# Attention scores whose second pass contracts 128 rows instead of 64

## The chip, the cores and the metric

The kernel runs on one core of a Trainium2 chip. The metric is the device time of one execution in microseconds (us). TensorE (PE) multiplies matrices; a matmul is two records, the load of its stationary operand (PEld, LDWEIGHTS) and the streaming of its moving operand (PE, MATMUL). VectorE (DVE), ScalarE (ACT) and GpSimd (POOL) do the rest, SyncE (SP) issues the weight loads.

## The reference, cut to what matters

Two layers of a diffusion backbone over 256 latent and 256 context tokens of width 1024. Each layer is a half-step SwiGLU feed-forward, a mixer, and another half-step feed-forward. The mixer has three branches on one projected input: grouped-query attention (A, 8 query heads of 64, 2 key heads), differential attention (B, 4 heads with two softmax maps each) and a Fourier mix (C). What the change touches is the scores:

```python
s = jnp.einsum('bqhgd,bkhd->bhgqk', q * HEAD_DIM ** -0.5, k)      # A, HEAD_DIM = 64
s = jnp.einsum('bqhmd,bkhmd->bhmqk', q * HEAD_DIM ** -0.5, k)     # B, two maps m
p = jax.nn.softmax(s, axis=-1)
```

Latent queries see 512 keys (context and latent), context queries see the 256 context keys. In the second layer the context has no queries.

## The kernel before

Every product is made of float32r parts: a float32 value is split into a high part (a cast on ACT) and a low part (a subtraction on DVE), and `mm3` (lines 305 to 307) multiplies high by high, high by low and low by high. Weights come through a stream (`WeightStream`, lines 202 and 203) that loads them and splits them ahead of their use.

The mixer's work on TensorE stands in an order written out at build time. `Interleave` keeps a clock of its own: large products (projections of six units, gates, branches) are run in the order of `PACE[l]["order"]`, and between them it puts the stages of small tasks whose operands its clock calls ready. Each stage yields its time on TensorE, its time on VectorE and a delay to the next stage (`sa`, `sb`, `tr`, ... in `PACE`). TensorE takes the result strictly in that order, so a stage that is put too early makes all products behind it wait.

Attention runs in units: two of branch A (4 query heads and 1 key head each) and four of branch B (2 query maps and 2 key maps each). `unit_post` normalises q and k, applies the rotation, and for each of the four token tiles of 128 writes two packs: pq has a query head as 128 columns [high, low] (in B's second map [low, high]), pk has a key head as [high, high] (`dup`), and after these the low part of k, 64 columns for each key head (`low`, line 651). Each pack of 128 columns is transposed on TensorE into a PSUM bank `att` (line 660) and copied by ACT (line 662) into a slot of the unit's stack, so that the 128 rows of a slot hold a head's 64 dimensions twice. The low part is transposed on its own (line 665): in A it has 64 columns and gives 64 rows, in B two heads of 64 columns give the two halves of 128 rows. A copy of its own on ACT (line 666) follows.

`scores` makes the scores of 128 queries and 512 or 256 keys in pairs of matmuls. The first (line 679) contracts 128 rows, [q high; q low] with [k high; k high]; the second (line 680) adds q high times k low and contracts the 64 rows in which q high lies:

```python
nc.tensor.matmul(d, qt, k, start=True, stop=False)                 # line 679
nc.tensor.matmul(d, qt[rows], low[rows], start=False, stop=True)   # line 680
```

Then DVE takes the negated maximum (line 683), ACT the exponential with its sum (line 686), DVE the reciprocal (line 687) and the scaling (line 710 in A; lines 746 to 748 in B). `spread` transposes the result (line 698), ACT and DVE split it into parts (lines 263 and 264), and TensorE multiplies it with v (line 723 in A, `mm3` in B).

Of the kernel before, what the change touches and what calls it, by code (L numbers as in the profile page):

```python
# [32 lines left out]
# z ** -0.5 on [0.9324, 1.0691], where the guess puts z, as a polynomial with the leading coefficient scaled to 1  # L33
# [29 lines left out]
class Slots:  # L63
    """buffers that a task holds over several of its stages"""
# [14 lines left out]
class Stack:  # L79
    """a unit's transposed operands: eight slots of the latent and the context tokens, in one buffer or in two"""  # L80
# [11 lines left out]
    def keys(self, i, half):  # L92
        """all keys that a query of half sees, in pieces"""
        if half == 1:
            return [self.half(i, 1)]
        return [self.half(i, 0), self.half(i, 1)] if self.whole is None else [self.whole[:, i, :]]
# [8 lines left out]
class Interleave:  # L105
    """Puts the stages of small tasks between the products of large ones, in the order in which their operands
    are due: a stage yields its time on TensorE and on VectorE, and the delay to the next; a large one the times
    alone, or the tasks that it needs."""
# [62 lines left out]
class WeightStream:  # L171
    """Weight pieces in the order of their use: loads of whole pieces and splits of their halves into two
    float32r parts run ahead."""
# [32 lines left out]
    def next(self, key):  # L206
        """the two parts of the next half of a piece, to be given back with done()"""
        i = self.used
        assert self.pieces[i // 2][0] == key, (self.pieces[i // 2][0], key)
        self.ahead()  # L210
        assert self.split > i
        self.used += 1
        return self._parts(i)[1:]
# [6 lines left out]
class Net:  # L220
# [37 lines left out]
    def region(self, tag, dt, name):  # L258
        """a shared 16 KB region for a new use"""
        return self.pool.tile([P, 8, 512], dt, name=f"{tag}_{name}", tag=tag)  # L260
# [5 lines left out]
    def urgent(self, on=True):  # L266
        """ahead of what was emitted shortly before"""
        return self.tc.high_priority(offset=URG) if on else nullcontext()

    def rsqrt(self, y, x, sums, n, t):  # L270
        """1 / sqrt(sums / n + EPS): a first guess from the exponent, then a polynomial in x * guess ** 2"""
        v = self.nc.vector
        v.tensor_scalar(x, sums, RSQRT_SCALE / n, RSQRT_SCALE * EPS, op0=ALU.mult, op1=ALU.add)
        v.tensor_scalar(y.bitcast(I32), x.bitcast(I32), -0.5, RSQRT_MAGIC, op0=ALU.mult, op1=ALU.add)
        v.tensor_tensor(t, y, y, op=ALU.mult)
        v.tensor_tensor(x, t, x, op=ALU.mult)
        v.scalar_tensor_tensor(t, x, RSQRT_POLY[3], x, op0=ALU.add, op1=ALU.mult)
        for c in RSQRT_POLY[2:0:-1]:
            v.scalar_tensor_tensor(t, t, c, x, op0=ALU.add, op1=ALU.mult)
        v.scalar_tensor_tensor(y, t, RSQRT_POLY[0], y, op0=ALU.add, op1=ALU.mult)  # L280

    def col_rsqrt(self, sq, n, dg):
        """sq [P, 256]: rsqrt(column sum / n + EPS) on all partitions, in PSUM"""
        self.col_scale(sq, n, dg)
        return self.spread_cols(dg)
# [24 lines left out]
    def cond_region(self, name, after=None):  # L310
        """silu of both conditioning vectors on all partitions, and room for the rows of w_ada"""
        nc = self.nc
        t = self.region("ya", F32, name)
        self.sil = t[:, 0:4, :].rearrange("p (c a) b -> p c (a b)", c=2)
        self.adaraw = [t[:, 4 + 2 * i:6 + 2 * i, :].rearrange("p a b -> p (a b)") for i in range(2)]
        self.bg_base = 0
        if after is not None:
            nc.gpsimd.tensor_copy(self.sil[:, 0, 0:1], after)
        nc.gpsimd.dma_start(self.sil, self.io["cc"])
        for c in range(2):  # L320
            s, u = self.sil[:, c, :], self.adaraw[c]
            nc.scalar.activation(u, s, AF.Tanh, scale=0.5)
            nc.vector.scalar_tensor_tensor(s, u, 1.0, s, op0=ALU.add, op1=ALU.mult)
# [6 lines left out]
    def bg_plan(self, n):  # L330
        """n rows of w_ada spread evenly over the coming feed-forward"""
        self.bg_n, self.bg_done, self.bg_time = n, 0, 0
        self.bg_total = 512 * (2 * NF + 2 * (KT - 3) + KT)
# [74 lines left out]
    def update(self, m, half, ps, g):  # L408
        """h += gate * ps"""
        c = _half(half)  # L410
        self.nc.vector.scalar_tensor_tensor(self.h[:, m, c], ps[:, c], g[:, m, half:half + 1], self.h[:, m, c],  # L411
                                            op0=ALU.mult, op1=ALU.add)
        self.fin(m, half)
# [140 lines left out]
    def unit_proj(self, l, u, kv_only, run, first, needs, post):  # L554
        """q, k and v of one unit for all token tiles; kv_only: no q for the context"""
# [25 lines left out]
    def unit_post(self, u, ps, c0s):  # L581
# [9 lines left out]
        # values  # L591
        for half in range(2):
            vs = self.raw[half][:, :, nh * HD:384]
            if is_a:
                vd = st.half(6, half).rearrange("p (t x d) -> p t x d", t=2, x=2)
                vd = [vd[:, :, i, :] for i in range(2)]
            else:
                vd = [st.half(5 + i, half).rearrange("p (t c) -> p t c", t=2) for i in range(2)]
            self.split(vd[0], vd[1], vs)
        # queries and keys  # L600
# [13 lines left out]
        kd, kl = (4, 5) if is_a else (2, 4)  # L614
        cost, lat = 7.0, self.pace["post"]
        for half in range(2):
# [16 lines left out]
            # transposed stacks: q [hi; lo], k [hi; hi], lo of k  # L633
            for tt in range(2):
# [14 lines left out]
                low = pk[:, nk * P:nk * P + nk * HD]  # L649
                nc.scalar.copy(dup, ks.unsqueeze(2).to_broadcast([P, nk, 2, HD]))  # L650
                nc.vector.tensor_tensor(low.rearrange("p (a d) -> p a d", d=HD), ks, _r(dup[:, :, 0, :]), op=ALU.subtract)
                cols += [(kd + i, pk[:, i * P:i * P + P]) for i in range(nk)]
                yield 0.0, cost, lat
                cost, lat = 0.5, self.pace["tt"]
                pe = (len(cols) + 1) * 0.08
# [7 lines left out]
                b = self.att.next()  # L663
                m = nk * HD
                nc.tensor.matmul(b[:m, 0:P], low, self.identr, start=True, stop=True)
                nc.scalar.copy(st.tok(kl, half, tt)[:m], b[:m, 0:P])
# [3 lines left out]
    def scores(self, half, st, q, kd, kl, rows, e, qts):  # L670
        """exp(S - max) [P q, keys] of query tiles qts, and 1 / sum; q, kd, kl: slots of st"""
# [3 lines left out]
        for x, i in enumerate(qts):  # L675
            qt, o = st.tok(q, half, i), x * n
            for k, low in zip(st.keys(kd, half), st.keys(kl, half)):
                d = ps[:, o:o + k.shape[-1]]
                nc.tensor.matmul(d, qt, k, start=True, stop=False)  # L679
                nc.tensor.matmul(d, qt[rows], low[rows], start=False, stop=True)  # L680
                o += k.shape[-1]
# [8 lines left out]
    def spread(self, half, es, pt):  # L690
        """transposes es, two [P q, keys], into pt"""
# [9 lines left out]
    def att_a(self, j, half, pr, e):  # L701
        nc = self.nc
        st = self.stack(j)
        rows = slice(0, HD)
# [3 lines left out]
        for x, qts in enumerate(((0,), (1,)) if half == 0 else ((0, 1),)):  # L708
            for p, rc in self.scores(half, st, 2 * pr + e, 4, 5, rows, slots[x], qts):
                nc.vector.tensor_scalar(p, p, rc, None, op0=ALU.mult)  # L710
                es.append(p)
# [14 lines left out]
        # the sum of the rows by the two parts of v  # L726
# [9 lines left out]
    def att_b(self, b, half):  # L736
# [5 lines left out]
        for qts in ((0,), (1,)) if half == 0 else ((0, 1),):  # L742
            slots = yield from self.ep.get(2)
            s = [self.scores(half, st, m, 2 + m, 4, slice(m * HD, m * HD + HD), slots[m], qts) for m in range(2)]
# [15 lines left out]
        for k in range(nk):  # L760
            kc = slice((k % 2) * 256, (k % 2) * 256 + 256)
            v = [st.tok(5 + x, half + k // 2, k % 2) for x in range(2)]
# [23 lines left out]
    def split_tables(self):  # L786
        """position tables in pt (hi 0,1, lo 2,3), channel tables in pt 4 (hi | lo)"""
# [6 lines left out]
    def uc_proj(self, l, halves, hn1):  # L794
        """u of branch C, token-major: hi in u1 0..3, lo in u1 4..7"""
# [24 lines left out]
    def fourier(self, g, half, s):  # L820
        """the sums over positions for the cosines and sines of frequencies 0..128 alone: tokens are ordered so that
        those of 255..128 mirror them"""
# [35 lines left out]
    def branch(self, l, i, y, mp, N, first, last, needs):  # L858
        """adds gate * (y @ w_branch) of two feature tiles to the merged sum"""
# [32 lines left out]
    def gates(self, l, mp, N):  # L892
        """the tanh of two feature tiles of branch B's gates, kept beside the merged sum"""
# [39 lines left out]
    def mixer_steps(self, l):  # L933
        """the large steps in order, with the weight pieces that each takes"""
# [95 lines left out]
    def start(self):  # L1030
        """loads; shift and scale of the first norm as (silu(c) @ w_ada) on the tensor engine"""
# [106 lines left out]
def _order():  # L1138
    """tokens 0..127, then 255..128"""
# [83 lines left out]
```

## Time and profile before

| what | value |
|---|---|
| median of 3 runs | 2172.9 us |
| lowest, highest | 2165.63, 2173.29 us |
| span of the profiled execution | 2166.2 us |
| PE, PEld busy in the span | 2135.8 us, 1819.9 us |
| DVE, ACT, POOL busy | 1486.5, 919.3, 113.8 us |
| matmuls | 11706 |

The profiled execution has no time of its own printed beside its span; the span is 6.7 us (0.3%) under the median of the runs and 0.6 us over the lowest. A line number such as L680 is the line of the kernel above. The start of a matmul is a record, its end is modelled, so two neighbouring matmuls overlap in the records, and the time from one start to the next is what a matmul takes of the engine.

### The profile page before, as it was taken

What the parts mean: (1) busy time and instruction counts of PE and PEld (TensorE: products, weight loads), DVE (VectorE), ACT (ScalarE), POOL (GpSimd) and SP (SyncE); (2) the same over time, 40 slices, a digit from 0 to 9 for tenths busy, and PEclk for the clock granted to TensorE, in tenths of its full rate; (3) what the DMA queues carried; (4) which work ended last, traced back from release to release, by engine and by line L of the source; (5) the groups of instructions that cost most, each with busy time, mean ns of one, the idle gap of its engine ahead of it and who ended that gap; (6) DMA issues with size and microseconds to landing.
All of it is one profiled execution on the core that took longest, in us unless ns stands there. A gap on an engine that the chain in (4) does not pass through costs nothing.

```text
span 2166.2 us, 31632 instructions
## 1 busy us (share of the span) xinstructions
PE 2135.8 (99%) x11706; PEld 1819.9 (84%) x11706; DVE 1486.5 (69%) x3102; ACT 919.3 (42%) x1920; POOL 113.8 (5%) x235
## 2 busy tenths in 40 slices
PE   8999999999999999999999999999999999999999
PEld 3888888898888878888888898888888889988999
DVE  5878777667777774676666568765556687877664
ACT  4323333356654543332333333233324576655553
POOL 2000001100000010000000000000010000000000
PEclk9999999999999999999999999999999899999999
DMA  7545555321112243244544425555553223444655
GB/s 290 190 154 193 172 166 174 94 90 61 59 61 67 81 146 101 68 166 136 165 139 144 145 73 201 175 175 174 167 161 119 83 86 98 134 166 157 186 184 146
DMA packets 84779, 300.49 MB, mean 139 GB/s; under 512 B 9872, under 2 KB 11024, under 8 KB 83088
## 3 DMA queue, kind: packets, MB, share of 16 engines
q1 hardware_dynamic: 62640, 219.29, 31.1%
q0 software_dynamic: 21984, 79.18, 11.7%
q8 instruction: 92, 1.51, 0.3%
q14 instruction: 63, 0.52, 0.1%
HBM read 293.19 MB, written 5.24 MB: 138 GB/s over the span
## 4 chain that ended last, share of the span: by engine, by line
PE 96%; DVE 2%; ACT 1%; DMA 1%; issue 0%; SPq 0%; ACTq 0%; DVEq 0%
PE mm L305 29%; PE mm L306 29%; PE mm L307 28%; PE att L680 2%; PE att L679 2%; PE mm L1056 1%; PE att L698 1%; PE att L660 1%; PE att L723 1%; DVE wlo L203 1%; PE att L299 1%; PE att L307 1%; PE att L305 0%; PE att L306 0%; PE att L291 0%; DMA wraw<-in_wout 0%
## 5 line engine op out<-in xcount | busy, mean ns | idle before, releaser
L202 ACT CAST whi<-wraw 128x512 fp32r<-128x512 f32 (+1 forms) x832 | 497.0, 600 | 919.9 <-PE mm L306 829.2
L203 DVE TENSOR_TENSOR wlo<-wraw,whi 128x512 fp32r<-128x512 f32 (+1 forms) x832 | 548.8, 664 | 360.7 <-ACT whi L202 356.5
L305 PE MATMUL mm<-hn,whi 128*128 128x512 f32 (+1 forms) x1888 | 666.0, 355 | 2.0 <-ACT hn L385 2.0
L306 PE MATMUL mm<-hn,whi 128*128 128x512 f32 (+1 forms) x1888 | 666.5, 354 | 0.0
L307 PE MATMUL mm<-hn,wlo 128*128 128x512 f32 (+1 forms) x1888 | 661.0, 351 | 0.0
L305 PEld LDWEIGHTS mm<-hn,whi 128*128 128x128 f32 x1888 | 355.9, 189 | 59.9 <-ACT hn L385 2.9
L307 PEld LDWEIGHTS mm<-hn,wlo 128*128 128x128 f32 x1888 | 356.7, 189 | 52.0
L306 PEld LDWEIGHTS mm<-hn,whi 128*128 128x128 f32 x1888 | 356.4, 189 | 49.9 <-DVE hn L386 0.2
L305 PE MATMUL mm<-whi,hn 128*128 128x384 f32 (+3 forms) x432 | 147.9, 342 | 0.7 <-DVE mg_m L884 0.6
L307 PE MATMUL mm<-whi,hn 128*128 128x384 f32 (+3 forms) x432 | 143.1, 331 | 0.3 <-DVE hn L386 0.3
L306 PE MATMUL mm<-wlo,hn 128*128 128x384 f32 (+3 forms) x432 | 143.0, 331 | 0.0
L352 DVE CUSTOM_DVE_ANT_0 gt<-ya_c,small 128x1024 bf16<-128x1024 f32 x113 | 142.9, 1280 | 0.0
L352 DVE CUSTOM_DVE_ANT_0 e<-ya_c,small 128x1024 bf16<-128x1024 f32 x111 | 140.5, 1280 | 0.8 <-DMA ya_c<-in_wada 0.8
L348 POOL DMA_DIRECT2D ya_c<-in_wada x128 | 67.8, 529 | 926.7 <-DVE ada L352 905.5
L305 PE MATMUL mm<-u_f,whi 128*128 128x256 f32 (+1 forms) x304 | 101.7, 335 | 0.0
L306 PE MATMUL mm<-u_f,whi 128*128 128x256 f32 (+1 forms) x304 | 101.6, 334 | 0.0
L307 PE MATMUL mm<-u_f,wlo 128*128 128x256 f32 (+1 forms) x304 | 100.7, 331 | 0.0
L411 DVE SCALAR_TENSOR_TENSOR h_h<-mm,gcol,h_h 128x256 f32<-128x256 f32 x104 | 49.9, 482 | 60.6 <-PE mm L307 59.9
L305 PEld LDWEIGHTS mm<-whi,hn 128*128 128x128 f32 x432 | 81.6, 189 | 6.9 <-issue 2.7
L307 PEld LDWEIGHTS mm<-whi,hn 128*128 128x128 f32 x432 | 81.5, 189 | 3.0 <-DVE hn L386 0.8
L306 PEld LDWEIGHTS mm<-wlo,hn 128*128 128x128 f32 x432 | 81.7, 189 | 2.2
L683 DVE TENSOR_REDUCE sm<-att 128x1 f32<-128x512 f32 (+1 forms) x80 | 54.5, 686 | 25.6 <-PE att L680 25.1
(261 smaller groups left out, 3248.3 us busy)
## 6 DMA issues: line engine op xcount, KB each, us to landing
wraw<-in_wi SPq DMA_DIRECT2D x176, 512.0 KB, 3.7
ya_c<-in_wada POOLq DMA_DIRECT2D x128, 512.0 KB, 3.9
wraw<-in_wo SPq DMA_DIRECT2D x64, 512.0 KB, 3.7
wraw<-in_gate SPq DMA_DIRECT2D x48, 512.0 KB, 3.5
wraw<-in_win SPq DMA_DIRECT2D x48, 384.0 KB, 3.1
wraw<-in_wo SPq DMA_DIRECT2D x32, 384.0 KB, 3.5
wraw<-in_wbr SPq DMA_DIRECT2D x24, 512.0 KB, 3.5
wraw<-in_wout SPq DMA_DIRECT2D x16, 512.0 KB, 3.6
```

The lines of the kernel that those rows point to most:

```text
L202: self.nc.scalar.copy(hi, raw)
L203: self.nc.vector.tensor_tensor(lo, raw, _r(hi), op=ALU.subtract)
L299: self.nc.tensor.matmul(bank, self.ones, dg, start=True, stop=True)
L305: mm(out, lh, rh, start=first, stop=False)
L306: mm(out, lh, rl, start=False, stop=False)
L307: mm(out, ll, rh, start=False, stop=last)
L348: self.nc.gpsimd.dma_start(self.adaraw[(self.bg_base + j) % 2], self.io["wada"][l, n])
L352: self.tc.keep_in_program_order(self.nc.vector.tensor_tensor_reduce(self.ft.next().bitcast(BF16), self.adaraw[self.bg_base % 2], self.sil[ ...
L411: self.nc.vector.scalar_tensor_tensor(self.h[:, m, c], ps[:, c], g[:, m, half:half + 1], self.h[:, m, c], op0=ALU.mult, op1=ALU.add)
L679: nc.tensor.matmul(d, qt, k, start=True, stop=False)
L680: nc.tensor.matmul(d, qt[rows], low[rows], start=False, stop=True)
L683: nc.vector.tensor_reduce(s[:, 0:w], ps[:, :w * n].rearrange("p (a b) -> p a b", a=w), axis=AX.X, op=ALU.max, negate=True)
```

## The change

The low half of k is written into the pack twice, as the high half is. It is then transposed together with the others: in A six packs of 128 columns in two banks (four and two), in B with queries six, without queries four. The separate transpose and its copy go. The key's low parts have slots of their own (A: 5, B: 4 and 5; B's values move to slots 6 and 7). The second matmul of a pair takes all 128 rows, which adds the product of both low parts to the scores. The planner's time for the transposes of a token tile goes from 0.08 to 0.11 per transpose. Elsewhere the diff takes out comments and docstrings.

```diff
-                vd = [st.half(5 + i, half).rearrange("p (t c) -> p t c", t=2) for i in range(2)]
+                vd = [st.half(6 + i, half).rearrange("p (t c) -> p t c", t=2) for i in range(2)]
...
-        kd, kl = (4, 5) if is_a else (2, 4)
+        kd = 4 if is_a else 2
...
-                low = pk[:, nk * P:nk * P + nk * HD]
-                nc.scalar.copy(dup, ks.unsqueeze(2).to_broadcast([P, nk, 2, HD]))
-                nc.vector.tensor_tensor(low.rearrange("p (a d) -> p a d", d=HD), ks, _r(dup[:, :, 0, :]), op=ALU.subtract)
-                cols += [(kd + i, pk[:, i * P:i * P + P]) for i in range(nk)]
+                low = pk[:, nk * P:2 * nk * P].rearrange("p (a x d) -> p a x d", a=nk, d=HD)
+                ks = ks.unsqueeze(2).to_broadcast([P, nk, 2, HD])
+                nc.scalar.copy(dup, ks)
+                nc.vector.tensor_tensor(low, ks, _r(dup), op=ALU.subtract)
+                cols += [(kd + i, pk[:, i * P:i * P + P]) for i in range(2 * nk)]
...
-                pe = (len(cols) + 1) * 0.08
+                pe = len(cols) * 0.11
...
-                b = self.att.next()
-                m = nk * HD
-                nc.tensor.matmul(b[:m, 0:P], low, self.identr, start=True, stop=True)
-                nc.scalar.copy(st.tok(kl, half, tt)[:m], b[:m, 0:P])
...
-                nc.tensor.matmul(d, qt[rows], low[rows], start=False, stop=True)
+                nc.tensor.matmul(d, qt, low, start=False, stop=True)
...
-            for p, rc in self.scores(half, st, 2 * pr + e, 4, 5, rows, slots[x], qts):
+            for p, rc in self.scores(half, st, 2 * pr + e, 4, 5, slots[x], qts):
...
-            s = [self.scores(half, st, m, 2 + m, 4, slice(m * HD, m * HD + HD), slots[m], qts) for m in range(2)]
+            s = [self.scores(half, st, m, 2 + m, 4 + m, slots[m], qts) for m in range(2)]
...
-            v = [st.tok(5 + x, half + k // 2, k % 2) for x in range(2)]
+            v = [st.tok(6 + x, half + k // 2, k % 2) for x in range(2)]
```

## Rows read from the trace of the kernel before

**Rows 1.** The page's first part: busy us, share of the span, instructions

```profile
PE 2135.8 (99%) x11706; PEld 1819.9 (84%) x11706; DVE 1486.5 (69%) x3102; ACT 919.3 (42%) x1920; POOL 113.8 (5%) x235
```

**Rows 2.** The page's fourth part: the chain that ended last, by engine

```profile
PE 96%; DVE 2%; ACT 1%; DMA 1%; issue 0%; SPq 0%; ACTq 0%; DVEq 0%
```

**Rows 3.** Windows (from:to, length, busy us of each engine, PEclk, DMA) of the mixers

```profile
480.00:800.00 320.00, 319.96 (x1658) 268.53 (x1657) 236.88 (x615) 181.99 (x458) 10.07 (x23) 0.99 0.23 70
640.00:660.00 20.00, 20.00 (x81) 14.52 (x81) 12.87 (x34) 10.80 (x32) 0.00 (x0) 0.91 0.10 24
1690.00:1720.00 30.00, 26.67 (x150) 22.66 (x149) 18.02 (x51) 16.30 (x46) 0.00 (x0) 0.77 0.23 73
1740.00:1920.00 180.00, 178.93 (x1294) 165.66 (x1294) 143.61 (x372) 117.18 (x284) 0.00 (x0) 1.00 0.35 107
```

**Rows 4.** Line 680 by tile: ns min/median/max, first and last start, forms

```profile
L680 PE MATMUL att<-u_m x88: 379/492/793, 496.1 to 1881.5; 64*128 64x512 f32 x56, 64*128 64x256 f32 x32
...
L680 PE MATMUL att<-ya_m x8: 378/382/385, 1816.6 to 1912.4; 64*128 64x256 f32 x8
...
L680 PE MATMUL att<-yb_m,ya_m x8: 379/381/382, 1817.3 to 1913.0; 64*128 64x256 f32 x8
```

**Rows 5.** Timeline of PE around scores over 512 keys: start, us, instruction

```profile
494.13 0.67 PE L660 MATMUL att<-identr,pack 128*128 128x128 f32 x5
494.64 0.22 PE L665 MATMUL att<-identr,pack 128*64 128x128 f32 x1
494.69 0.39 PE L305 MATMUL mm<-whi,hn 128*128 128x384 f32 x1
...
495.62 0.34 PE L307 MATMUL mm<-whi,hn 128*128 128x384 f32 x1
495.80 0.39 PE L679 MATMUL att<-u_m 128*128 128x512 f32 x1
496.12 0.49 PE L680 MATMUL att<-u_m 64*128 64x512 f32 x1
...
498.69 0.49 PE L680 MATMUL att<-u_m 64*128 64x512 f32 x1
...
499.39 0.34 PE L306 MATMUL mm<-wlo,hn 128*128 128x384 f32 x1
```

**Rows 6.** Timeline of PEld there; in brackets idle time before and its end

```profile
495.62 0.19 PEld L679 LDWEIGHTS att<-u_m 128*128 128x128 f32 x1
496.11 0.18 PEld L680 LDWEIGHTS att<-u_m 64*128 64x128 f32 x1 [0.30 <-issue]
```

**Rows 7.** Timeline of PE, scores over 256 keys

```profile
532.05 0.38 PE L679 MATMUL att<-u_m 128*128 128x256 f32 x1
...
533.61 0.38 PE L680 MATMUL att<-u_m 64*128 64x256 f32 x1
```

**Rows 8.** Timeline of PE, a large product with 512 columns

```profile
652.66 0.40 PE L307 MATMUL mm<-hn,wlo 128*128 128x512 f32 x1
...
653.36 0.39 PE L307 MATMUL mm<-hn,wlo 128*128 128x512 f32 x1
```

**Rows 9.** Timeline of PE, eight products with 256 columns in a row

```profile
555.90 1.10 PE L723 MATMUL att<-pt_m,u_m 128*128 128x256 f32 x8
556.83 0.34 PE L305 MATMUL mm<-whi,hn 128*128 128x384 f32 x1
```

**Rows 10.** Lines 665 and 651 by tile, with their forms

```profile
L665 PE MATMUL att<-identr,pack x48: 219/274/356, 482.7 to 1902.9; 128*128 128x128 f32 x32, 128*64 128x128 f32 x16
...
L651 DVE TENSOR_TENSOR pack<-h_m,pack x48: 204/284/295, 477.6 to 1900.3; 128x128 fp32r<-128x128 f32 x32, 128x64 fp32r<-128x64 f32 x16
```

**Rows 11.** Timeline of all engines where scaled scores are transposed

```profile
503.35 0.48 DVE L710 TENSOR_SCALAR e<-e,sm 128x512 f32<-128x512 f32 x1
...
504.37 0.27 PE L698 MATMUL att<-ident,e 128*128 128x128 f32 x1
```

More of the change, by code (lines that the diff above doesn't have):

```diff
@@ L662, in unit_post, with scores @@
                     nc.scalar.copy(st.parts[half][:, s0:s0 + len(now), c], b[:, :len(now) * P].rearrange("p (a c) -> p a c", c=P))
-                b = self.att.next()
-                m = nk * HD
-                nc.tensor.matmul(b[:m, 0:P], low, self.identr, start=True, stop=True)
-                nc.scalar.copy(st.tok(kl, half, tt)[:m], b[:m, 0:P])
                 yield pe, 0.0, 0.3
             cost, lat = 0.004 * 2 * ns[1] * HD, self.pace["h1"]
-    def scores(self, half, st, q, kd, kl, rows, e, qts):
+    def scores(self, half, st, q, kd, kl, e, qts):
         nc = self.nc
@@ L703, in att_a @@
         st = self.stack(j)
-        rows = slice(0, HD)
         w = 2 - half
```

## The prediction

> **What bounds the kernel now.** I read the page's busy shares first. PE is busy 99% of the span, and no other engine more than 84% [rows 1]. The chain that ended last is PE for 96% [rows 2], so what shortens PE's stream shortens the kernel, as long as the operands are there in time. The busy share hides something, though: a matmul's end is modelled, and a matmul that starts late still overlaps its neighbour in the records. So I went on to the windows of the mixers, and from there to the timeline, and measured from start to start.
>
> Scores over 512 keys: from the first second-pass matmul (496.12) to the last (498.69) lie six steps in 2.57 us, 0.428 us each [rows 5]. A large product with the same 512 columns takes 0.70 us for three steps, 0.233 each [rows 8]. Scores over 256 keys: five steps from 532.05 to 533.61, 0.312 each [rows 7]; eight products with 256 columns take 0.93 us, 0.116 each [rows 9]. So each score matmul takes some 0.195 us more than its columns ask for, whether long or short.
>
> The weight loads tell where that time goes. The load for the first score matmul starts at 495.62, beside the matmul of line 307 that starts then. The load for the 64-row matmul starts only at 496.11, after 0.30 us in which the loading side stood idle and waited for nothing that the profile shows ("issue") [rows 6]; its matmul follows at 496.12 [rows 5]. Where 128 rows follow 128 rows the load is hidden; where the row count changes it isn't. A pair changes it twice, once into 64 rows and once back.
>
> It isn't the accumulation into one bank: `mm3` accumulates three matmuls into one bank at 0.233 [rows 8]. Nor is it a stationary operand with fewer columns: after the 64-column transpose the next matmul starts 0.05 us later (494.64 to 494.69), sooner than the 0.102 us that each 128-column transpose before it takes (five in 0.51) [rows 5].
>
> **The change part by part.**
>
> *Second pass with 128 rows.* There are 56 second-pass matmuls over 512 keys and 32 + 8 + 8 = 48 over 256 [rows 4], with as many first-pass ones. If all follow one another like the large products: 56 x 2 x (0.428 - 0.233) = 21.8 us, and 48 x 2 x (0.312 - 0.116) = 18.8 us, together 40.6 us. A check on a whole block: from the first score matmul (495.80) to the second large one behind the block (499.39) lie 3.59 us [rows 5]; eight steps of 0.233 and one like 495.62 to 495.80 make 2.04, so 1.55 less, 0.194 for each of eight. That is the upper bound; below, no row excludes that the stall stays (rival 2). I take 40.6, since everywhere that 128 rows follow 128 rows the load is hidden.
>
> The Trainium skill, TensorEngine Tiling (Array Packing), section Key Properties, says that a change of tiling mode drains TensorE. The trace agrees for rows. It lists 128x64 as a mode too; by that the 16 transposes of 64 columns [rows 10] would cost two drains each, and their removal would give some 6 us more. The 0.05 us behind such a transpose [rows 5] says that they cost none.
>
> *Transposes.* Of the 48 separate ones, 32 had 128 columns (branch B, two heads at once) and become two [rows 10]: 32 x 0.102 = 3.3 us more [rows 5]. The 16 of branch A had 64 columns and become 128 wide: 16 x (0.102 - 0.05) = 0.8 more. PE: +4.1. That nothing has 64 columns any more is a small loss here.
>
> *Packing on DVE.* Line 651 takes 204 ns with 64 columns and 284 with 128 [rows 10], 80 more for each 64. A: 16 x 0.08; B to 256 columns: 32 x 0.16; together 6.4 us. It is hidden while DVE has room: in the two large mixer windows it is busy 236.9 + 143.6 = 380.5 of 500 us [rows 3]. With 6.4 more and 36.5 us less time (40.6 - 4.1) that is 387 of 463, 83%. Without that cover it costs the 6.4.
>
> *PSUM copies on ACT.* A tile of A with queries has two copies instead of three; in B the copy of 128 columns becomes one of 256. ACT is busy 57% to 65% in these windows [rows 3]; I take nothing, at worst a few tenths of a microsecond per unit.
>
> *Order.* The planner's times for the transposes grow by 0.06 to 0.26 per tile, so some stages move by a product or so. No row prices this; the waits it can make or spare are in the next two terms.
>
> *What is late next.* The stage after the scores is the transposing of the scaled scores. PE now comes to it up to 1.55 us sooner, while the maximum, exponential and scaling go on at the pace of DVE and ACT. In the tightest group the last scaling ends at 503.83 and the first transpose that reads it starts at 504.37 [rows 11]: 0.54 us, so up to 1.0 us of wait there. Matching scalings with transposes in order, 8 of 32 groups have less than 1.55 us; their bound is 8 x 1.0 = 8 us. Below it is 0, since DVE starts sooner too (its maximum waits for line 680). I take 2.5, near the low end, because the other seven have more room. Behind a waiting transpose all products on PE wait, and then the weight buffers that they free.
>
> *Clock.* TensorE's granted clock has two levels, 1.2 and 2.4 GHz. The mean is 0.91 in 640 to 660, with scores at its start, and 0.77 in 1690 to 1720, where PE sat idle 3.33 us [rows 3]. These are (1 - 0.91)/0.5 x 20 = 3.6 and (1 - 0.77)/0.5 x 30 = 13.8 us at the half level, half of which is lost: 1.8 and 6.9. A stream without stalls can spare the first and shorten the second: between 0 and 8.7; a new wait can bring another. I take 1, since the second has its own idle time, which the change doesn't touch.
>
> Sum: 40.6 - 4.1 - 2.5 + 1 = 35 us off. The sum stands against the span of the profiled execution, 2166.2, and gives 2131.2; its own time isn't shown, and the median of the runs lies 6.7 over it. Against the median: 2172.9 - 35 = 2138.
>
> **The rivals.**
>
> 1. *DVE and ACT hold the mixers.* PE runs ahead and gives back half at the transposes and at the split weights: 2172.9 - 17.5 = 2155. For it: DVE at 83%, ACT in between, groups with 0.54 us of room [rows 11]. Against it: PE idled only 0.04 us in 320 [rows 3]. 13%.
>
> 2. *The stall isn't the change of rows*, and the score matmuls keep their 0.428 and 0.312; only 4.1 us come on top: 2177. Against it are the large products and the loads hidden beside them. 4%. The Trainium skill, TensorE: Matmul & The Clock Gate, section The mechanism, says that loads overlap running matmuls only where the row groups differ. By that rule two 128-row passes would stall as well and this rival would hold; the load at 495.62 [rows 6], beside a matmul of the same 128 rows [rows 5], speaks against it.
>
> 3. *Slower: operands too late and the clock falls.* If the shifted order puts stages before their operands, PE idles as at 1690 to 1720: 3.3 us of waiting and 6.9 us at the half clock, 10.2 for such a place. It decides above (36.5 + 10.9)/10.2 = 4.6 places; five give 2172.9 - 36.5 + 51 = 2187. Against it: the windows of [rows 3] have one such place, and the transposes' shift is small. 6%.
>
> **How the numbers follow.** My forecast has 77%, its own range 2124 (the full 40.6, most of the 8.7 and no waits) to 2152 (8 us of waits, 6.4 us of DVE without cover, no clock). About 0.5%, 10.9 us, is what a measurement of this kernel can tell. Rival 1 lies mostly beyond it: faster 77 + 11 = 88%, same 2 + 4 = 6%, slower 6%. The range reaches to rival 1 with some room: 2124 to 2160; outside stay rivals 2 and 3 and a few per cent of the rest.
>
> **What would show it.** Starts of score matmuls 0.23 us apart with 512 keys and 0.12 with 256, with no idle "issue" time before their loads. 32 more matmuls (11738), line 665 gone, the low part's subtraction at some 284 and 444 ns. Waits of PE for DVE at the transposes of a few microseconds. The prediction is wrong if the steps stay at 0.4 and 0.3, or if PE idles at many transposes, or if the clock falls at new places.

## The result, and the profile after

The changed kernel takes 2130.55 us (median of 4 runs, 2129.1 to 2132.27) against 2170.59 us before (4 runs). The ratio is 0.9816, with a 95% interval of 0.9805 to 0.9828: some 40 us less. The profiled executions' spans, 2129.1 and 2166.2 us, differ by 37.1. Part of the 40 is the granted clock, which differs from one execution to the next: at the same mean clock, on one chip (the runs beside experiment 5), the changed kernel took 2131.9 us against 2168.2 and 2168.9 (0.994), and 2129.8 and 2130.9 against 2165.4 and 2166.7 (0.995), some 36 us less.

The page's first part answers to [rows 1]:

```profile
PE 2097.2 (99%) x11738; PEld 1818.2 (85%) x11738; DVE 1487.2 (70%) x3102; ACT 918.4 (43%) x1896; POOL 114.8 (5%) x235
```

PE is busy 99% again, though its busy time is 38.6 us shorter, with 32 matmuls more. The busy share could not show the stall before and cannot show now that it has gone. The timeline of PE around the same scores, 512 keys and then 256, answers to [rows 5, 7]; the second pass is now line 677, the transposes are line 661:

```profile
494.80 0.78 PE L661 MATMUL att<-identr,pack 128*128 128x128 f32 x6
495.42 0.39 PE L305 MATMUL mm<-whi,hn 128*128 128x384 f32 x1
...
496.51 0.39 PE L676 MATMUL att<-u_m 128*128 128x512 f32 x1
496.74 0.40 PE L677 MATMUL att<-u_m 128*128 128x512 f32 x1
...
498.11 0.40 PE L677 MATMUL att<-u_m 128*128 128x512 f32 x1
...
529.45 0.28 PE L676 MATMUL att<-u_m 128*128 128x256 f32 x1
...
530.04 0.28 PE L677 MATMUL att<-u_m 128*128 128x256 f32 x1
```

Six steps in 1.37 us are 0.228 each (0.428 before), five in 0.59 are 0.118 (0.312 before). Six transposes of 128 columns take 0.62 us, 0.103 each. The load side there (PEld, answers to [rows 6]) follows without a pause:

```profile
496.52 0.19 PEld L677 LDWEIGHTS att<-u_m 128*128 128x128 f32 x1
496.75 0.19 PEld L676 LDWEIGHTS att<-u_m 128*128 128x128 f32 x1
```

The load for the second pass runs beside the matmul of the first; the 0.30 us of "issue" has gone.

What PE idles, and the granted clock, by the windows of both kernels (from:to, length, busy us and count of PE, PEld, DVE, ACT and POOL, PEclk, DMA). First the kernel before, three windows that its rows above don't have:

```profile
440.00:480.00 40.00, 39.78 (x242) 37.30 (x241) 24.59 (x61) 20.45 (x50) 0.00 (x0) 1.00 0.23 74
1690.00:1920.00 230.00, 224.59 (x1560) 204.40 (x1559) 174.77 (x449) 144.74 (x358) 0.00 (x0) 0.97 0.33 103
...
1960.00:2000.00 40.00, 34.95 (x269) 33.98 (x269) 29.25 (x66) 20.05 (x41) 0.00 (x0) 0.91 0.44 145
```

Then the changed kernel, the answers to these and to [rows 3]:

```profile
440.00:760.00 320.00, 319.38 (x1829) 290.06 (x1828) 247.93 (x637) 193.70 (x486) 8.71 (x19) 1.00 0.23 73
640.00:660.00 20.00, 20.00 (x119) 18.06 (x118) 15.20 (x45) 8.80 (x22) 0.00 (x0) 1.00 0.19 54
1670.00:1700.00 30.00, 25.62 (x169) 23.90 (x168) 19.75 (x55) 17.24 (x46) 0.00 (x0) 0.89 0.33 101
1670.00:1880.00 210.00, 203.06 (x1537) 198.27 (x1536) 170.27 (x437) 140.72 (x335) 0.00 (x0) 0.98 0.36 111
...
1920.00:1960.00 40.00, 34.95 (x262) 33.97 (x261) 28.36 (x64) 19.56 (x40) 0.00 (x0) 0.87 0.43 141
2100.00:2129.10 29.10, 25.38 (x216) 25.17 (x214) 10.74 (x17) 7.30 (x12) 0.00 (x0) 0.97 0.35 102
```

The mixer of the first layer starts at the same time in both kernels, so both are read from 440. PE idles 0.62 + 6.94 = 7.6 us in the two mixers, against 0.22 + 0.04 + 5.41 = 5.7 before: 1.9 more. What the half clock costs is the missing share of the clock times the window. Near 645 us it has gone. At the head of the second layer's mixer it costs (1 - 0.89) x 30 = 3.3 us instead of 6.9. Behind that mixer and at the end of the kernel it costs 5.2 + 0.9 instead of 3.6.

### The profile page after: what moved, and what is told of

It reads as the page before. It is cut to its first block, busy times and chain, and to the rows that moved or that the text cites. A ratio compares the mean times of both kernels' runs of the same rounds, so it can differ in the third digit from the quotient of the medians.

```text
span 2129.1 us, 31670 instructions
## 1 busy us (share of the span) xinstructions
PE 2097.2 (99%) x11738; PEld 1818.2 (85%) x11738; DVE 1487.2 (70%) x3102; ACT 918.4 (43%) x1896; POOL 114.8 (5%) x235
## 3 DMA queue, kind: packets, MB, share of 16 engines
q0 software_dynamic: 21984, 79.18, 11.8%
## 4 chain that ended last, share of the span: by engine, by line
PE 95%; DVE 2%; ACT 1%; DMA 1%; issue 0%; SPq 0%; ACTq 0%; DVEq 0%
PE mm L305 29%; PE mm L306 29%; PE mm L307 28%; PE mm L1052 1%; PE att L661 1%; PE att L695 1%; PE att L676 1%; PE att L677 1%; PE att L719 1%; DVE wlo L203 1%; PE att L299 1%; PE att L307 1%; PE att L305 0%; PE att L306 0%; PE att L291 0%
## 5 line engine op out<-in xcount | busy, mean ns | idle before, releaser
L306 PE MATMUL mm<-mg_f,whi 128*128 128x512 f32 (+1 forms) x204 | 72.1, 353 | 0.0
```

Source lines behind the costliest of these rows:

```text
L306: mm(out, lh, rl, start=False, stop=False)
```

## The experiments

All are set against runs of the kernel before on the same chip: a median of 2170.4 us (17 runs) for experiments 1 to 4 and of 2170.7 us (9 runs) for experiment 5.

**1. The second pass back to 64 rows, all else as changed** (`rows64_back`). The order of instructions on PE, DVE and ACT is that of the changed kernel. The edit that counts (the calls of `scores` hand over the rows again):

```diff
-                nc.tensor.matmul(d, qt, low, start=False, stop=True)
+                nc.tensor.matmul(d, qt[rows], low[rows], start=False, stop=True)
```

> The changed kernel, but the second pass contracts 64 rows again; packs, transposes, slots, planner times and the order on every engine are those of the changed kernel. If the change of the row count between neighbouring matmuls costs the time: steps of 0.428 and 0.312 us are back, 104 pairs x 2 x 0.2 us, so 2130.5 + 41 = 2171 us, within 6 us of the kernel before. If the gain came from the wider transposes or from the new order of stages: it stays, 2131 us. If the 64-column transposes had cost drains of their own (some 6 us less than the kernel before, by the mode count, and 4 us more for the wider ones): 2165 to 2169.

It took 2178.04 us (median of 12 runs), a ratio of 1.0025 (1.0012 to 1.0037) to the kernel before. The whole gain is gone, so it belongs to the row count of the second pass alone. The timeline of PE:

```profile
497.90 0.49 PE L677 MATMUL att<-u_m 64*128 64x512 f32 x1
498.32 0.50 PE L676 MATMUL att<-u_m 128*128 128x512 f32 x1
...
500.48 0.49 PE L677 MATMUL att<-u_m 64*128 64x512 f32 x1
```

Six steps in 2.58 us: 0.43 each, as before. The expectation was 2171. Five of the twelve executions came out there, 2170.5 to 2172.9 us at a mean granted clock of 0.994; the other seven took 2178.0 to 2181.1 at 0.989 to 0.991. The profile is of one of these seven (2177.7 us, 0.990), and its windows show where the clock is lost:

```profile
0.00:50.00 50.00, 40.36 (x119) 12.12 (x120) 23.83 (x75) 18.73 (x43) 10.45 (x35) 0.93 0.76 298
640.00:660.00 20.00, 20.00 (x73) 14.19 (x72) 12.44 (x33) 9.62 (x28) 0.00 (x0) 0.83 0.13 40
1670.00:1720.00 50.00, 46.92 (x284) 42.40 (x283) 32.87 (x92) 28.19 (x73) 0.00 (x0) 0.86 0.23 72
1740.00:1760.00 20.00, 18.94 (x101) 14.30 (x102) 16.25 (x38) 13.96 (x35) 0.00 (x0) 0.90 0.17 52
1870.00:1900.00 30.00, 29.10 (x203) 26.63 (x202) 25.02 (x64) 20.01 (x48) 0.00 (x0) 0.94 0.38 121
```

The windows from 640, 1740 and 1870 have their falls at blocks of scores; they cost (1 - 0.83) x 20 = 3.4 us, 2.0 and 1.8, where the changed kernel's profile has 1.00. Behind waits of 1.06 and 0.90 us for the key's slots (line 676 for line 663) the clock falls within the block of scores, at 1756 and 1879 us; the changed kernel has the same two waits and keeps the full clock. The 7.0 us in 1670 to 1720 lie behind PE's waits at the head of the second layer's mixer, as the 6.9 of the kernel before do. The first 50 us cost 3.5 instead of 1.5 (0.93 against 0.97), and no scores stand there, so these 2 us are not the row changes. None of the eight runs of the changed kernel has a mean clock under 0.994. So with the row changes back the clock fell further in seven executions of twelve; why not in the other five, and what part of it the changes cause, stays open.

The new packs cost a little: the five runs stand some 3 us above the seven runs of the kernel before at the same 0.994 (2168.1 to 2169.5). That is near the 4.1 of the wider transposes. There are no 64-column transposes in this kernel; had each cost two drains before, it would stand some 2 us below (6 less, 4.1 more). The 64-column transposes cost no drain that the time shows.

**2. Half as many row changes, in the kernel before** (`snake`). Every second pair runs its second pass first.

```diff
-                nc.tensor.matmul(d, qt, k, start=True, stop=False)
-                nc.tensor.matmul(d, qt[rows], low[rows], start=False, stop=True)
+                self.pair = 1 - self.pair
+                for y, (a, b) in enumerate([(qt, k), (qt[rows], low[rows])][::1 - 2 * self.pair]): nc.tensor.matmul(d, a, b, start=y == 0, stop=y == 1)
```

> The kernel before with the two passes of every second pair swapped: 128, 64, 64, 128 rows instead of 128, 64, 128, 64. As many 64-row matmuls, but half as many changes of the row count (104 instead of 208). If each change costs 0.196 us: 104 x 0.196 = 20 us less, 2150. If each 64-row matmul costs 0.39 us, whatever stands beside it: no change, 2170. If a 64-row matmul behind another of the same rows cannot hide its load: 2160 to 2170, with steps of 0.4 between two 64-row matmuls.

It took 2145.36 us, ratio 0.988 (0.9866 to 0.9895): 25 us less, where 20 were expected. At the same mean clock of 0.994 it is 2145.0 to 2146.2 against 2168.1 to 2169.5, 23 us less. All 104 64-row matmuls are still there, so the cost goes with the changes and not with the 64-row matmul. The timeline of PE, a block of branch A:

```profile
496.99 2.81 PE L680 MATMUL att<-u_m 128*128 128x512 f32 x8
499.63 0.34 PE L305 MATMUL mm<-whi,hn 128*128 128x384 f32 x1
```

The two passes now share a line, so eight score matmuls are merged into one row. They take 2.64 us with four changes; eight undisturbed steps of 0.228 take 1.82. That leaves 0.20 us per change, the price of the prediction. In the trace's records all neighbours in this block start 0.32 to 0.34 us apart, two 64-row matmuls on the same rows too: half of a change's price falls on the step into it and half on the next step. The 0.4 us between 64-row matmuls of the third expectation did not come. More than the price of 104 changes was saved in branch B's blocks, where the second passes of the two maps stand next to each other and use rows 0 to 63 and rows 64 to 127:

```profile
645.66 1.26 PE L680 MATMUL att<-u_m 128*128 128x512 f32 x4
646.76 0.40 PE L305 MATMUL mm<-hn,whi 128*128 128x512 f32 x1
```

Four matmuls and two changes take 1.10 us, where half of the A block takes 1.32. Windows of 0.03 us count the instructions that are under way, first just behind the start of the two 64-row loads of that block, then in the block of branch A:

```profile
645.97:646.00 0.03, 0.03 (x3) 0.02 (x2) 0.00 (x0) 0.00 (x0) 0.00 (x0) 1.00 0.00 0
...
497.32:497.35 0.03, 0.03 (x2) 0.03 (x1) 0.00 (x0) 0.03 (x1) 0.00 (x0) 1.00 0.50 205
```

In the B block three matmuls are under way at once, with two loads beside them; in the A block two and one. In the records the two 64-row matmuls of such a block start 3 to 4 ns apart: on different halves of the rows they run side by side. Twelve such blocks over 512 keys (four units of the first layer and two of the second, two query tiles each) save 12 x 0.22 = 2.6 us. With the 20 us of the changes that makes 23, what the runs at the same clock show.

**3. No second pass** (`one_pass`). Leaves out the product with the low part of k.

```diff
-                nc.tensor.matmul(d, qt, k, start=True, stop=False)
-                nc.tensor.matmul(d, qt, low, start=False, stop=True)
+                nc.tensor.matmul(d, qt, k, start=True, stop=True)
```

> The changed kernel without the second pass: the product with the low part of k is left out. If TensorE's stream sets the time of the mixers still, the 56 matmuls of 512 and 48 of 256 columns come off in full, 56 x 0.228 + 48 x 0.117 = 18 us: 2112. If DVE and ACT have become the bound there: under 5 us, 2126 to 2131, with PE waiting for DVE at the transposes of the scaled scores.

It took 2119.01 us, 11.5 less than the changed kernel, between the two expectations. Who waits for whom, PE alone, 496 to 752 us (total, times, longest):

```profile
PE att L661 <- DVE pack L264: 1.2, 1, 1.2
PE att L718 <- DVE pt_m L264: 0.7, 1, 0.7
PE att L694 <- DVE h_m L705: 0.5, 1, 0.5
PE att L661 <- ACT h_m L682: 0.2, 1, 0.2
```

With another 18 us out of PE's stream, waits come up in the first layer, most of them for DVE: at the packs, at the split scores and at the scaled scores. In the changed kernel PE waits 0.3 us there. Behind the longest one, which ends at 575 us, the clock falls to the half level for a while:

```profile
560.00:580.00 20.00, 18.56 (x88) 14.66 (x87) 18.62 (x52) 13.25 (x32) 0.00 (x0) 0.93 0.16 49
580.00:600.00 20.00, 20.00 (x129) 19.08 (x129) 14.09 (x34) 13.07 (x38) 0.00 (x0) 0.98 0.17 54
```

That costs 1.4 + 0.4 us; the changed kernel has 1.00 in both. Some waits show as idle only in part, since the modelled end of the matmul before covers their beginning: the 0.5 us in front of line 694 is 0.63 from start to start. With each step set against the median step between the same shapes in the changed kernel, late starts and half clock make 5.9 us more in the mixer of the first layer, nearly all of the 6.5 that are missing. So the changed kernel is near the point where DVE takes a share of the bound.

**4. The planner's old times for the transposes** (`old_plan_times`).

```diff
-                pe = len(cols) * 0.11
+                pe = (len(cols) - nk + 1) * 0.08
```

> The changed kernel with the planner's old times for the transposes of a token tile (0.48 and 0.40 instead of 0.66), so that only the order of the small stages differs. If the order is worth nothing to speak of: 2128 to 2133. If the new times brought part of the gain by fewer waits: 2135 or more. If they cost waits: 2126 or less.

It took 2129.0 us (2127.78 to 2131.0), as the first expectation says. Some stages stand elsewhere on PE, but the time is the same within the scatter: the new planner times neither brought nor cost anything that can be measured.

**5. The changed kernel once more, and two versions that might beat it.** In branch B, where two low parts already fill 128 columns, the second copy can be left out: the 64 rows of the other map then add a product of two low parts of different maps, a term that is no part of the scores but is as small as the product of the low parts that it replaces. `b_low_once_g0` moves the first gates step besides.

> The changed kernel once more, beside the two below: 2130 us, within 3.

```diff
-                low = pk[:, nk * P:2 * nk * P].rearrange("p (a x d) -> p a x d", a=nk, d=HD)
+                low = pk[:, nk * P:nk * P + P].rearrange("p (x d) -> p x d", d=HD)
...
-                cols += [(kd + i, pk[:, i * P:i * P + P]) for i in range(2 * nk)]
+                cols += [(kd + i, pk[:, i * P:i * P + P]) for i in range(nk + 1)]
...
-            s = [self.scores(half, st, m, 2 + m, 4 + m, slots[m], qts) for m in range(2)]
+            s = [self.scores(half, st, m, 2 + m, 4, slots[m], qts) for m in range(2)]
```

> The changed kernel, but in branch B the low parts of the two key maps stand once, side by side, in one pack of 128 columns, as before the change; the second pass still contracts 128 rows. The rows of the other map add a product of two low parts of different maps, in the place of that of the same map. 32 transposes go (32 x 0.102 = 3.3 us of PE) and 5 us of DVE. If TensorE's stream sets the time: 2127. If the mixers hang on DVE as well: 2123 to 2126. If the order that follows brings new waits: 2130 or more.

> As b_low_once, and in the second layer the first gates step stands between the first two projections, so that TensorE has work while DVE and ACT pack the first unit. If the waits of 2.0 and 0.7 us there and the half clock of 6.8 us behind them go: 2.7 + 3.4 = 6 us less than b_low_once, 2121. If the stages that lose the gates step as a filler later wait instead: no gain, 2127 or more.

The changed kernel took 2130.33 us, `b_low_once` 2127.56 (2125.9 to 2129.27; ratio to before 0.9803, 0.979 to 0.9816), as its first expectation says. The medians differ by 2.8 us and the spans by 3.3, which is the price of 32 transposes; the intervals of the two ratios overlap, so the gain is not clear of the scatter. `b_low_once_g0` differs from it by one edit:

```diff
-        dict(order="u0 p0 p1 c0 p2 c1 c2 p3 a0 c3 p4 g0 p5 g1 ...
+        dict(order="u0 p0 g0 p1 c0 p2 c1 c2 p3 a0 c3 p4 p5 g1 ...
```

It took 2133.15 us, 5.6 more than `b_low_once`. Who waits for whom, PE alone:

```profile
PE att L299 <- DVE h_m L295: 2.6, 1, 2.6
PE att L664 <- ACT pack L651: 2.6, 3, 1.5
...
PE att L698 <- DVE pt_m L264: 1.4, 1, 1.4
```

The 2.0 us wait at the head of the second layer's mixer (PE for the pack of line 264) has gone, but the stages that lost the gates step wait instead: the last normalisation 2.6 us instead of 1.1, the packs 2.6 instead of 0.9, a split 1.4 instead of 0.6. The second expectation held.

## Why the prediction was right, step by step

*The stall at every change of rows* was right, in place and size. Predicted were 40.6 us; measured are 56 x 2 x (0.428 - 0.228) + 48 x 2 x (0.312 - 0.118) = 41.0. These steps are read from one block of each kind. Over all 30 blocks of the kernel before, the score matmuls and the one behind them take 44.7 us more than undisturbed steps, some 3 of them at the half clock; in the changed kernel it is 1.7. Experiment 1 shows that it is the row count and nothing else in the change, and experiment 2 that it is the change from one count to the other, 0.20 us each.

*The transposes* cost what was said, 0.103 us each, 4.1 in all. That a stationary operand of 64 columns has no drain was read from one step of 0.05 us; experiment 1 bears it out. By the page that was weighed there (the Trainium skill, TensorEngine Tiling (Array Packing), Key Properties) a change of mode drains TensorE. That holds here for 64 rows, with 0.20 us, and not for 64 columns.

*The waits* were taken at 2.5 us in a range of 0 to 8; PE idles 1.9 us more in the mixers. The size was right by luck, for they are not where the prediction put them. PE's waits for the key's slots, in the kernel before, the changed kernel and the one with 64 rows back:

```profile
PE att L679 <- ACT u_m L662: 0.3, 1, 0.3
...
PE att L680 <- ACT u_m L666: 0.2, 1, 0.2
```

```profile
PE att L676 <- ACT u_m L663: 2.0, 2, 1.1
```

```profile
1754.52 0.49 PE L676 MATMUL att<-u_m 128*128 128x512 f32 x1 [1.06 <-ACT u_m L663]
```

Scores wait 1.5 us more for ACT's copies of the transposed packs, which the prediction put at nothing. The shorter stream is not the reason: with 64 rows back the two waits are there too (1.06 and 0.90 us), and with the planner's old times they are 2.2 us. At the transposes of the scaled scores, where the prediction expected the waits, PE waits for no scaling. Why not can be seen in the group of [rows 11]. The same two rows in the changed kernel, in the timelines of DVE and of PE:

```profile
502.51 0.49 DVE L706 TENSOR_SCALAR e<-e,sm 128x512 f32<-128x512 f32 x1
```

```profile
503.57 0.27 PE L695 MATMUL att<-ident,e 128*128 128x128 f32 x1
```

From the first score matmul of the block PE now needs 7.06 us to that transpose (503.57 - 496.51) instead of 8.57 (504.37 - 495.80). But the last scaling also ends sooner, 6.49 us behind it instead of 8.03, and the room is 0.57 us instead of 0.54. The chain on DVE and ACT hung on PE: its maxima wait for the second pass (25.1 us in 36 waits before, 11.8 in 16 after), and the weight splits in between wait for buffers that PE frees. The prediction's lower bound, that DVE moves along, was the better one at this place.

*The clock* was taken at 1 us in a range of 0 to 8.7. The mixers spare 1.8 + 3.6 = 5.4 us of it, the end of the second mixer and of the kernel give back 2.5; 2.9 net, in the profiled executions; between the medians it is some 4 (see the result). *DVE's 6.4 us* measured 5.5 (18.2 us at line 652 against 12.7 at line 651) and stayed hidden.

The sum with the measured terms is 41.0 - 4.1 - 1.9 + 2.9 = 37.9, against 37.1 between the spans and 40.0 between the medians; predicted were 35. Without the clock it is 35.0, against some 36 between runs at the same clock. That 2130.55 lies 7.5 under the forecast of 2138 has two reasons: the clock, taken at 1, and the median before, 2172.9 from three runs and 2170.59 with the fourth. Of the rivals, the first (half is given back) is refuted by the 40 us (36 at the same clock), the second (the row change is not the cause) by experiments 1 and 2. The third asked for five places where the order lets PE idle; the one such place of before is still the only large one.

## What to carry to other kernels

Read TensorE by the time from start to start, and by idle time of the load side: a busy share of 99% held a stall of 41 us. A matmul that contracted 64 rows between neighbours of 128 cost 0.2 us on the way in and as much on the way out here. Duplicating the operand so that neighbours had the same count was much cheaper (4.1 us of transposes against 41), and ordering them for half as many changes brought half. When a stream gets shorter on the engine that bounds, look at whether the chain that must keep up hangs on that engine; here it did, moved along, and the waits stayed small. Compare executions at the same granted clock before a few microseconds are given a cause.

## What the runs showed of the hardware that was not expected

- Two 64-row matmuls on different halves of the rows, into different banks, ran side by side: 1.10 us for a block that takes 1.32 when both use the same half (experiment 2).
- With the row changes back in an otherwise unchanged kernel the mean granted clock was 0.989 to 0.991 in seven executions of twelve and 0.994 in five; without them it was 0.994 to 0.997 in eight (experiment 1). The seven took some 7 us more than the five. What part of that the row changes cause is not shown.
- At half the clock the steps of score matmuls with changes grow too, from 0.43 to 0.72 us (1757.15 - 1756.43), in the kernel with 64 rows put back:

```profile
1756.43 0.79 PE L676 MATMUL att<-u_m 128*128 128x512 f32 x1
1757.15 0.79 PE L677 MATMUL att<-u_m 64*128 64x512 f32 x1
```
